# Tiles at byte 128 mod 512, and the latents' squares added some steps ahead of their sum

## The chip, the cores and the metric

The kernel runs on one core of a Trainium2 chip. The metric is the time of one execution on the device, in microseconds, as the median of three runs. One execution was also taken by the hardware profiler; all rows below come from it.

## What is computed

Two stacked models over 256 tokens of width 1024, all in float32. The reference, cut to its order:

```
h = x + gated_deltanet(rmsnorm(x))                 # 16 heads, chunks of 64
h = h + conv_gated_mlp(rmsnorm(h))                 # feed-forward 0, width 2816
k, v = shared_kv(h)
h = h + sliding_window_sink_attention(rmsnorm(h), k, v)
h = h + conv_gated_mlp(rmsnorm(h))                 # feed-forward 1
x = rmsnorm(h)
# second model
p = rms_norm(x) @ w_in           # linear attention q, k, v, gate; latents c_q (384), c_kv (256)
y_a = gla_branch(...) @ w_o_gla
y_b = mla_branch(rms_norm(c_q), rms_norm(c_kv), ...) @ w_o_mla
x = x + rms_norm((g_a * y_a + g_b * y_b) @ w_out)
x = x + rms_norm((silu(h @ w_fg) * (h @ w_fu)) @ w_fd)
```

Each latent is normalized by the root of the mean of its squares.

## The kernel before

**Matmuls.** Every float32 operand of a large product is held as two float32r parts, high and low, and a product is three matmuls into the same PSUM bank (`mm3`, lines 250 to 252): high x high, high x low, low x high. The first operand given is loaded into the array, the second one is moved through it. `gemm` loads weights (128 x 128) and moves activations of 256 columns (`xh`, `xl`; `fh`, `fl`; `ah`, `al`; `oh`, `ol`). `gemm_nat` and the last block's `down` load activations and move weights of 512 columns. Each such matmul loads its own operand, while the matmul before it is running.

**Weights.** All weights lie in one array `wall` of 362 tiles of 128 x 1024 float32, in the order of use. `_raw` (line 169) fetches a tile over SyncE's queue, `_prep` (line 176) splits it: ScalarE copies to `wh` (line 187), VectorE subtracts for `wl` (line 188). `w` (line 231) prepares two tiles ahead of the one in use (`LA = 2`), and each of `wr`, `wh`, `wl` has four buffers of 4,096 B per partition.

**Steps.** Work beside the matmuls (norms, attention, scans) is written as generators. `w` counts column tiles of weights; after each four of them `tick` lets every generator run to its next `yield`. So a `yield` is a distance of 12 matmuls of 256 columns in TensorE's order. The program is traced in that order, a scheduler orders the instructions of each engine by it, and each engine runs its own queue in order.

**Memory.** On-chip memory is handed out by pools, one behind the other in the order in which they are opened (`run`, line 557 on): `cp` (constants: `cols` of 592 float32, `ident` and `ones` of 128), `wp` (weights' buffers), `hp` (`h`), `sp` (small tiles, squares, row vectors), `xp` (`xh`, `xl`), then a stage's own pool: `gp` (delta rule), `xp2` and `fp0` (feed-forward 0), `sw` (attention), `lp`, `fp1` (feed-forward 1), `mp` (the second model's mixer), `f2` (its feed-forward). Within a pool tiles follow each other by tags; a tile takes its size per partition, rounded up to 32 B, times its buffers. `sp`, for example, holds `sqa` (2,048 B), `sq` (2 x 2,048), `dg` (1,024), `rsy` (4 x 256), `rst` (2 x 256), `rowb` (2 x 1,024), and some twenty pieces of 32 B, 11,296 B in all.

**Feed-forward 0 and 1** run the same function `ffn` (line 1033). After the fourth group of up-projections it alternates 48 matmuls of the up-projection (into `pb`) with 24 that accumulate the down-projection into `acc` (`acc_k`, moving operands `ah`, `al`). The pool holds three `fpad` (128 x 516 float32), then in feed-forward 0 `tbl` (64 B) and `oneh` (1,536 B), in feed-forward 1 three tiles of 1,024 B for the position tables, then `fy`, `ah`, `al`.

**The mixer's opening** (`mixer`, line 1291). `lat` (line 1338) writes the latents' squares by ScalarE (line 1342), two latents of 128 for `c_kv` (`sql[0]`, `sql[1]`), three for `c_q`. The generator `lat_stage` (line 1431) adds them up on VectorE (lines 1436, 1444, 1445), `colsum` (line 362) sums them over the partitions by TensorE with a column of ones (line 367), `rstd` makes the reciprocal root by a chain of small VectorE operations, `rows` turns it into a row by TensorE (line 453). The generator `la_stage` (line 1393) runs beside it: `rope` (line 1378), two pairs of gate matmuls (line 1404) with a `yield` after each, then logarithm, exponential and scan by ScalarE and VectorE, up to `e4`. The keys' generator multiplies by `e4` (line 1467) and transposes on TensorE (line 1473).

Of the kernel before, what the change touches and what calls it, by code (L numbers as in the profile page):

```python
# [2 lines left out]

# [1 line left out]

# [4 lines left out]
F32 = mybir.dt.float32  # L10
F32R = mybir.dt.float32r
BF16 = mybir.dt.bfloat16
I32 = mybir.dt.int32
AF = mybir.ActivationFunctionType
ALU = mybir.AluOpType
# [4 lines left out]
P = 128  # L20
# [24 lines left out]
NCOL = sum(v[1] for v in COLS.values())  # L45
# [62 lines left out]

CW = _cw_terms()

WARM = (5, 1, 3)
# [29 lines left out]
class Builder:  # L143
    LA = 2

    def __init__(self, tc, a, spec, dbg=None, upto=99):
        self.tc, self.nc, self.a, self.spec, self.dbg, self.upto = tc, tc.nc, a, spec, dbg, upto
        self.n = 0
        self.halves = {}
        self.raws = {}  # L150
        self.sides = []
        self.ticks = 0
        self.ready = True
        self.evq = []
        self.cs = None
        self.pins = {}
        self.extra = ()
# [399 lines left out]
    def run(self):  # L557
        nc, tc = self.nc, self.tc
        with ExitStack() as es:
            self.cp = es.enter_context(tc.tile_pool(name="cp", bufs=1))  # L560
            self.wp = es.enter_context(tc.tile_pool(name="wp", bufs=2))
            self.hp = es.enter_context(tc.tile_pool(name="hp", bufs=1))
            self.sp = es.enter_context(tc.tile_pool(name="sp", bufs=2))
            self.xp = es.enter_context(tc.tile_pool(name="xp", bufs=1))
            self.dp = es.enter_context(tc.tile_pool(name="dp", bufs=1, space=DRAM))
            self.ps = es.enter_context(tc.tile_pool(name="ps", bufs=8, space=PSUM))
            self.h = self.hp.tile([P, KD, T], F32, name="h")
            self.cols = self.cp.tile([P, NCOL], F32, name="cols")
            self.ident = self.cp.tile([P, P], F32, name="ident")
            for b in range(4):  # L570
                nc.sync.dma_start(self.h[:, 2 * b : 2 * b + 2], self.a["xT"][:, 2 * b : 2 * b + 2])
            nc.sync.dma_start(self.ident, self.cst("ident"))
            self._raw(0)
            nc.sync.dma_start(self.cols, self.a["cols"])
            self.ones = self.cp.tile([P, P], F32, name="ones")
            nc.gpsimd.memset(self.ones, 1.0)
            self.gdn()
            if self.upto < 2:
                return
            with tc.tile_pool(name="xp2", bufs=1) as self.xp2:  # L580
                self.ffn(0)
                if self.upto < 3:
                    return
                self.swa()
            if self.upto < 4:
                return
            with tc.tile_pool(name="lp", bufs=1) as self.lp:
                self.block2_consts()
                self.ffn(1)
                if self.upto < 5:  # L590
                    return
                self.block2()
# [6 lines left out]
    def gdn(self):  # L599
        nc, tc, sp = self.nc, self.tc, self.sp  # L600
        x = self.newx()
        self.sqs = []
        with tc.tile_pool(name="gp", bufs=1) as gp:

            wb = self.bank("warm")
            warm = lambda n, r: [nc.tensor.matmul(wb[:, 0 : r.shape[1]], self.ones, r, start=True, stop=True) for _ in range(n)]
            warm(WARM[0], self.ones)
            for b in range(4):
                self.add_sq(self.sqs, "sqa", b, lambda o: nc.scalar.activation(o, self.h[:, 2 * b : 2 * b + 2], AF.Square))
            cs = self.colsum(self.sqs)  # L610
            if PRE0:
                self._prep(0)
            rc = self.rstd(cs, D)
            warm(WARM[1], self.sqs[0])
            rb = self.rows(rc, psum=True)
            warm(WARM[2], self.h[:, 0])
            for i in range(8):
                t = gp.tile([P, T], F32, tag="t2", bufs=8, name="xn")
                op = nc.vector.scalar_tensor_tensor(t, self.h[:, i], self.col("a_norm", i), rb, ALU.mult, ALU.mult)
                nc.scalar.activation(x[0][:, i], t, AF.Copy)  # L620
                nc.vector.tensor_tensor(x[1][:, i], t, x[0][:, i].bitcast(F32), ALU.subtract)  # L621
                if i in PINS:
                    self.pins[PINS[i]] = op
                    self._prep(PINS[i])
            self.gdn_body(gp, x)
# [407 lines left out]
    def ffn(self, layer):  # L1033
        nc, tc, sp = self.nc, self.tc, self.sp
        x = self.x
        self.stats_rows(D)
        with tc.tile_pool(name=f"fp{layer}", bufs=1) as fp:
            padded = [fp.tile([P, 2, 2 + T], F32, tag=f"fpad{i}", name=f"fpad{i}") for i in range(3)]
            for t in padded:
                nc.gpsimd.memset(t[:, :, 0:2], 0.0)  # L1040
# [63 lines left out]
    def swa(self):  # L1104
        nc, tc, sp = self.nc, self.tc, self.sp
        xk, xq = self.x
        self.stats(D)
        with tc.tile_pool(name="sw", bufs=1) as ap:
            self.swa_body(ap, xk, xq)

    def swa_body(self, ap, xk, xq):
# [137 lines left out]

    def block2(self):  # L1250
        nc, tc, sp = self.nc, self.tc, self.sp
        with tc.tile_pool(name="mp", bufs=1) as mp:
            xm = self.mixer(mp)
        self.ffn2(xm)

# [34 lines left out]
    def mixer(self, mp):  # L1290
        nc, sp = self.nc, self.sp
# [41 lines left out]
        sql = [None] * 5  # L1333
# [97 lines left out]
        def lat_stage():  # L1431
            while sql[1] is None:
                yield
            for _ in range(3):
                yield
            nc.vector.tensor_tensor(sql[0], sql[0], sql[1], ALU.add)
            c = self.colsum(sql[0:1])
            nc.vector.tensor_tensor(rkv, self.rstd(c, 256, rc), rc, ALU.mult)
            yield
            rk_["b"] = self.rows(rkv)  # L1440
            st["rkv"] = 1
            while sql[4] is None:
                yield
            nc.vector.tensor_tensor(sql[2], sql[2], sql[3], ALU.add)
            nc.vector.tensor_tensor(sql[2], sql[2], sql[4], ALU.add)
            for _ in range(3):
                yield
            c = self.colsum(sql[2:3])
            nc.vector.scalar_tensor_tensor(rqs, self.rstd(c, 384, rc), 192 ** -0.5, rc, ALU.mult, ALU.mult)
            st["rqs"] = 1  # L1450

        self.side(la_stage())
        self.side(lat_stage())
        list(self.gemm("w_c", x, KD, [4, 0, 1, 2], evac_c))

# [284 lines left out]
    def ffn2(self, xm):  # L1740
        nc, tc, sp = self.nc, self.tc, self.sp
        stt = nc.vector.scalar_tensor_tensor
        with tc.tile_pool(name="f2", bufs=1) as fp:
            wrow = fp.tile([P, 2, D], F32, tag="wrow", name="wrow")
            nc.gpsimd.dma_start(wrow, self.a["wrow"].to_broadcast([P, 2, D]))
            mw = fp.tile([P, 2, D], F32, tag="mw", name="mw")
# [269 lines left out]
```

## Time and profile before

| | |
|---|---|
| median of 3 runs | 1205.18 us (1204.91 to 1206.57) |
| the profiled execution | 1206.04 us, span 1204.2 us |
| TensorE busy | 1166.8 us (97%), 9,308 matmuls |
| VectorE busy | 896.5 us (74%) |
| ScalarE busy | 689.4 us (57%) |
| weights moved | 362 x 512 KB, mean 171 GB/s over the span |

A matmul's record lasts longer than its distance to the next one, since matmuls are pipelined: a row of 0.28 us may be followed 0.12 us later by the next. So the cost of a matmul in a stream is read from starts, and busy time in a window is the time in which at least one is under way. The granted clock is given as a share of 2.4 GHz; 0.5 is 1.2 GHz.

### The profile page before, as it was taken

The numbers are of one execution on the slowest core, as the hardware profiler recorded it, in microseconds if no ns is written. First come the engines' busy times: TensorE is split into PE (matmuls) and PEld (weight loads), VectorE is DVE, ScalarE is ACT, GpSimd is POOL, SyncE is SP. The second block draws the span as 40 slices with busy tenths as digits, with TensorE's granted clock in tenths as the row PEclk, the third lists the DMA queues.
The fourth block names the chain that finished last, engine by engine and source line by source line (L and its number), as shares of the span: only waits on it lengthen the run. The fifth ranks groups of instructions, "written<-read, shape, count | busy, mean of one in ns | idle before, by whom it ended". The sixth has DMA issues, their size and how long they took to land.

```text
span 1204.2 us, 23264 instructions
## 1 busy us (share of the span) xinstructions
PE 1166.8 (97%) x9308; PEld 1102.7 (92%) x9308; DVE 896.5 (74%) x1645; ACT 689.4 (57%) x1172; POOL 24.7 (2%) x46
## 2 busy tenths in 40 slices
PE   6999999999999999989999999799999999999997
PEld 6989888999999999889999998689789998999996
DVE  5968977669877879879987879546666667665565
ACT  4786556546655556656655557546465555444443
POOL 2000000000000001000000000000000000000000
PEclk9999999999999999999999999799999999999999
DMA  6546375455665657435656555244245664566562
GB/s 211 191 134 202 120 224 179 140 164 164 218 191 190 187 189 244 132 101 172 196 190 192 183 186 177 70 156 142 88 150 184 192 216 153 174 191 188 185 192 86
DMA packets 68204, 206.00 MB, mean 171 GB/s; under 512 B 18085, under 2 KB 18229, under 8 KB 67840
## 3 DMA queue, kind: packets, MB, share of 16 engines
q1 hardware_dynamic: 65488, 194.77, 51.3%
q0 software_dynamic: 2608, 9.75, 2.3%
q8 instruction: 73, 1.20, 0.4%
q14 instruction: 35, 0.29, 0.1%
HBM read 199.75 MB, written 4.74 MB: 170 GB/s over the span
## 4 chain that ended last, share of the span: by engine, by line
PE 81%; DVE 11%; ACT 3%; issue 2%; DMA 1%; SPq 0%; DVEq 0%; ACTq 0%; POOLq 0%
PE pb L250 18%; PE pb L251 18%; PE pb L252 18%; PE acc L250 6%; PE acc L252 6%; PE acc L251 6%; DVE wl L188 3%; DVE cy L705 1%; DMA NT<-s 1%; DVE TI L817 1%; DVE fst L815 1%; ACT wh L187 0%; DMA ident<-cst 0%; ACT S L1178 0%; DVE fy L1053 0%
## 5 line engine op out<-in xcount | busy, mean ns | idle before, releaser
L188 DVE TENSOR_TENSOR wl<-wr,wh 128x1024 fp32r<-128x1024 f32 x362 | 441.9, 1223 | 193.7 <-ACT wh L187 192.8
L187 ACT ACTIVATE wh<-wr 128x1024 fp32r<-128x1024 f32 x362 | 381.7, 1057 | 319.6 <-issue 88.2
L250 PE MATMUL pb<-xh,wh 128*128 128x256 f32 x1224 | 346.4, 283 | 0.6 <-ACT xh L620 0.6
L251 PE MATMUL pb<-xl,wh 128*128 128x256 f32 x1224 | 343.1, 280 | 0.3 <-DVE xl L621 0.2
L252 PE MATMUL pb<-xh,wl 128*128 128x256 f32 x1224 | 342.8, 281 | 0.2 <-DVE wl L188 0.2
L250 PEld LDWEIGHTS pb<-xh,wh 128*128 128x128 f32 x1224 | 231.2, 189 | 3.1 <-issue 1.6
L251 PEld LDWEIGHTS pb<-xl,wh 128*128 128x128 f32 x1224 | 231.3, 189 | 0.9 <-DVE xl L621 0.4
L252 PEld LDWEIGHTS pb<-xh,wl 128*128 128x128 f32 x1224 | 231.0, 189 | 0.4 <-DVE wl L188 0.4
L250 PE MATMUL pb<-fh,wh 128*128 128x256 f32 x416 | 116.9, 282 | 0.0
L251 PE MATMUL pb<-fl,wh 128*128 128x256 f32 x416 | 116.1, 279 | 0.5 <-DVE fl L471 0.4
L252 PE MATMUL pb<-fh,wl 128*128 128x256 f32 x416 | 115.8, 279 | 0.0
L252 PE MATMUL acc<-ah,wl 128*128 128x256 f32 x352 | 98.1, 279 | 0.4 <-DVE wl L188 0.4
L251 PE MATMUL acc<-al,wh 128*128 128x256 f32 x352 | 98.2, 279 | 0.0
L250 PE MATMUL acc<-ah,wh 128*128 128x256 f32 x352 | 98.1, 279 | 0.0
L251 PEld LDWEIGHTS pb<-fl,wh 128*128 128x128 f32 x416 | 78.3, 188 | 1.5 <-DVE fl L471 0.8
L250 PEld LDWEIGHTS pb<-fh,wh 128*128 128x128 f32 x416 | 78.1, 188 | 1.3 <-issue 0.4
L252 PEld LDWEIGHTS pb<-fh,wl 128*128 128x128 f32 x416 | 78.2, 188 | 0.0
L1053 DVE SCALAR_TENSOR_TENSOR fy<-fpad,cols,fy 128x256 f32<-128x256 f32 x176 | 73.4, 478 | 0.0
L250 PE MATMUL pb<-wh,xh 128*128 128x512 f32 (+1 forms) x176 | 70.9, 405 | 0.0
L251 PE MATMUL pb<-wl,xh 128*128 128x512 f32 (+1 forms) x176 | 68.9, 391 | 1.5 <-DVE wl L188 1.5
L252 PE MATMUL pb<-wh,xl 128*128 128x512 f32 (+1 forms) x176 | 68.5, 389 | 0.0
L252 PEld LDWEIGHTS acc<-ah,wl 128*128 128x128 f32 x352 | 66.2, 188 | 0.6 <-DVE wl L188 0.6
(455 smaller groups left out, 2082.0 us busy)
## 6 DMA issues: line engine op xcount, KB each, us to landing
wr<-wall SPq DMA_DIRECT2D x362, 512.0 KB, 3.8
wzd<-zt POOLq DMA_DIRECT2D x8, 256.0 KB, 2.8
wzog<-wzd POOLq DMA_DIRECT2D x4, 512.0 KB, 4.3
bias<-bd POOLq DMA_DIRECT2D x4, 512.0 KB, 6.8
h<-xT SPq DMA_DIRECT2D x4, 256.0 KB, 4.1
h<-xT POOLq DMA_DIRECT2D x1, 1024.0 KB, 7.8
wrow<-wrow POOLq DMA_DIRECT2D x1, 1024.0 KB, 9.4
out_dram<-mw SPq DMA_DIRECT2D x4, 256.0 KB, 2.0
```

Of the source, the lines that this page charges most:

```text
L187: nc.scalar.activation(hi, r, AF.Copy)
L188: i = nc.vector.tensor_tensor(lo, r, hi.bitcast(F32), ALU.subtract)
L250: mm(out, ah, bh, start=start, stop=False, skip_group_check=skip)
L251: mm(out, ah, bl, start=False, stop=False, skip_group_check=skip)
L252: mm(out, al, bh, start=False, stop=stop, skip_group_check=skip)
L705: nc.vector.scalar_tensor_tensor(y[:, i, n:], u[:, : T - n], w(j), y[:, i, n:], ALU.mult, ALU.add)
L815: nc.vector.tensor_tensor(tmp, NT[:, j, j + 1 :].unsqueeze(2).to_broadcast([P, m, j + 1]), TI[:, j, 0 : j + 1].unsqueeze(1).to_broadcast([ ...
L817: nc.vector.tensor_tensor(TI[:, j + 1 :, 0 : j + 1], TI[:, j + 1 :, 0 : j + 1], tmp, ALU.add)
L1053: nc.vector.scalar_tensor_tensor(y[:, i], u[:, i, j : j + T], w(j), y[:, i], ALU.mult, ALU.add)
```

## The change

A class `Split` takes the place of most pools: a tile of 1,024 B or more goes to one pool, rounded up to a multiple of 512 B, a smaller one to a second pool behind it, which is filled up to a multiple of 512 B at the end. The tile that is used keeps its shape. `cols` gets 48 more columns, of which nothing is used. In `lat_stage` the first addition moves ahead of the yields, and both sums stand four yields later in place of three.

```diff
+LINE = 512
+class Split:
+    def __init__(self, big, small, nbufs):
+        self.big, self.small, self.nbufs, self.tags = big, small, nbufs, {}
+
+    def tile(self, shape, dtype, **kw):
+        item = 2 if dtype == BF16 else 4
+        n = math.prod(shape[1:])
+        if n * item < 1024:
+            self.tags[kw.get("tag", kw.get("name"))] = -(-n * item // 32) * 32 * kw.get("bufs", self.nbufs)
+            return self.small.tile(shape, dtype, **kw)
+        unit = LINE // item
+        m = -(-n // unit) * unit
+        if m == n:
+            return self.big.tile(shape, dtype, **kw)
+        t = self.big.tile([shape[0], m], dtype, **kw)[:, :n]
...
+    def fill(self, rest):
+        n = (rest - sum(self.tags.values())) % LINE
+        if n:
+            self.small.tile([P, n // 4], F32, tag="fill", bufs=1, name="fill")
+
+@contextmanager
+def split_pool(tc, name, bufs, rest=0):
+    with tc.tile_pool(name=name, bufs=bufs) as big, tc.tile_pool(name=name + "s", bufs=bufs) as small:
+        p = Split(big, small, bufs)
+        yield p
+        p.fill(rest)
...
-            self.sp = es.enter_context(tc.tile_pool(name="sp", bufs=2))
-            self.xp = es.enter_context(tc.tile_pool(name="xp", bufs=1))
+            self.sp = es.enter_context(split_pool(tc, name="sp", bufs=2, rest=0))
+            self.xp = es.enter_context(split_pool(tc, name="xp", bufs=1))
...
-            self.cols = self.cp.tile([P, NCOL], F32, name="cols")
+            self.cols = self.cp.tile([P, NCOL + 48], F32, name="cols")[:, :NCOL]
...
         def lat_stage():
             while sql[1] is None:
                 yield
-            for _ in range(3):
-                yield
             nc.vector.tensor_tensor(sql[0], sql[0], sql[1], ALU.add)
+            for _ in range(4):
+                yield
             c = self.colsum(sql[0:1])
...
             nc.vector.tensor_tensor(sql[2], sql[2], sql[3], ALU.add)
             nc.vector.tensor_tensor(sql[2], sql[2], sql[4], ALU.add)
-            for _ in range(3):
+            for _ in range(4):
                 yield
             c = self.colsum(sql[2:3])
```

The pools `xp2`, `lp`, `gp`, `fp0`, `fp1`, `sw`, `mp` and `f2` become split pools in the same way.

## Rows read from the trace of the kernel before

**Rows 1.** windows: start:end us, length, busy us (count) per engine, granted clock, DMA share, GB/s

```profile
272.00:462.00 190.00, 190.00 (x1635) 189.16 (x1634) 161.99 (x259) 117.17 (x182) 4.49 (x7) 1.00 0.60 191
746.00:750.20 4.20, 1.43 (x10) 1.26 (x8) 3.42 (x11) 2.62 (x6) 0.00 (x0) 0.87 0.55 164
750.20:769.50 19.30, 19.30 (x115) 16.96 (x114) 10.31 (x41) 11.55 (x16) 0.00 (x0) 0.76 0.20 60
769.50:778.50 9.00, 0.27 (x4) 0.06 (x2) 7.82 (x12) 3.62 (x4) 0.00 (x0) 0.70 0.48 158
```

**Rows 2.** waits of TensorE: engine, line, releaser, us in total, times, longest

```profile
PE kdt L1473 <- DVE kd L1467: 8.7, 1, 8.7
PE csum L367 <- DVE sql L1436: 2.8, 1, 2.8
```

**Rows 3.** windows of the matmuls into `acc` alone, feed-forward 0 and 1

```profile
272.00:462.00 190.00, 63.08 (x528) 1.00 0.60 191
541.00:729.00 188.00, 65.77 (x528) 1.00 0.59 186
```

**Rows 4.** timeline of TensorE, feed-forward 0 and 1: start us, us, instruction

```profile
300.79 0.28 PE L250 MATMUL acc<-ah,wh 128*128 128x256 f32 x1
302.83 0.28 PE L250 MATMUL acc<-ah,wh 128*128 128x256 f32 x1
...
569.85 0.28 PE L250 MATMUL acc<-ah,wh 128*128 128x256 f32 x1
571.62 0.28 PE L250 MATMUL acc<-ah,wh 128*128 128x256 f32 x1
```

**Rows 5.** timeline of TensorE, the output product of the linear attention

```profile
970.14 0.28 PE L250 MATMUL pb<-goh,wh 128*128 128x256 f32 x1
975.74 0.28 PE L250 MATMUL pb<-goh,wh 128*128 128x256 f32 x1
```

**Rows 6.** groups by line and shape, TensorE: instruction, count, busy us, mean ns, idle before

```profile
L250 PE MATMUL pb<-xh,wh 128*128 128x256 f32 x1224 | 346.4, 283 | 0.6 <-ACT xh L620 0.6
L250 PE MATMUL pb<-fh,wh 128*128 128x256 f32 x416 | 116.9, 282 | 0.0
L250 PE MATMUL pb<-wh,xh 128*128 128x512 f32 x160 | 66.2, 416 | 0.0
L250 PE MATMUL acc<-oh,wh 128*128 128x256 f32 x192 | 55.1, 291 | 2.0 <-ACT oh L467 2.0
```

**Rows 7.** timeline of TensorE, 512-column matmuls of the last block

```profile
993.55 0.40 PE L250 MATMUL pb<-wh,xh 128*128 128x512 f32 x1
995.65 0.40 PE L250 MATMUL pb<-wh,xh 128*128 128x512 f32 x1
...
1095.22 0.39 PE L250 MATMUL acc<-wh,ah 128*128 128x512 f32 x1
1096.36 0.39 PE L252 MATMUL acc<-wh,al 128*128 128x512 f32 x1
```

**Rows 8.** groups by line, VectorE, 272 to 462 us, then 541 to 729 us

```profile
L1053 DVE SCALAR_TENSOR_TENSOR fy<-fpad,cols,fy 128x256 f32<-128x256 f32 x88 | 36.7, 477 | 0.0
...
L1053 DVE SCALAR_TENSOR_TENSOR fy<-fpad,cols,fy 128x256 f32<-128x256 f32 x88 | 36.7, 479 | 0.0
```

**Rows 9.** timeline of ScalarE at the latents' squares

```profile
747.43 0.64 ACT L1342 ACTIVATE sql<-pb 128x256 f32<-128x256 f32 x2
```

**Rows 10.** chain that ended last, 745 to 780 us: start us, us, step

```profile
747.56 1.23 DVE wl L188
748.78 0.35 DVE sql L1436
749.27 0.98 PE csum L367 x4
759.64 1.07 PE gate L1404 x4
778.49 1.11 PE kdt L1473 x4
```

More of the change, by code (lines that the diff above doesn't have):

```diff
@@ L1 @@
 import math
-from contextlib import ExitStack
+from contextlib import ExitStack, contextmanager
 import numpy as np
@@ L109 @@
 CW = _cw_terms()
+LINE = 512
[13 more added lines that the diff above has]
+        t = self.big.tile([shape[0], m], dtype, **kw)[:, :n]
+        if len(shape) == 2:
+            return t
+        ax = "abc"[: len(shape) - 1]
+        return t.rearrange("p (" + " ".join(ax) + ") -> p " + " ".join(ax), **dict(zip(ax, shape[1:])))
+    def fill(self, rest):
[8 more added lines that the diff above has]
+        p.fill(rest)
 WARM = (5, 1, 3)
@@ L579, in run @@
                 return
-            with tc.tile_pool(name="xp2", bufs=1) as self.xp2:
+            with split_pool(tc, name="xp2", bufs=1) as self.xp2:
                 self.ffn(0)
@@ L586, in run @@
                 return
-            with tc.tile_pool(name="lp", bufs=1) as self.lp:
+            with split_pool(tc, name="lp", bufs=1) as self.lp:
                 self.block2_consts()
@@ L602, in gdn @@
         self.sqs = []
-        with tc.tile_pool(name="gp", bufs=1) as gp:
+        with split_pool(tc, name="gp", bufs=1) as gp:
             wb = self.bank("warm")
@@ L1036, in ffn @@
         self.stats_rows(D)
-        with tc.tile_pool(name=f"fp{layer}", bufs=1) as fp:
+        with split_pool(tc, name=f"fp{layer}", bufs=1) as fp:
             padded = [fp.tile([P, 2, 2 + T], F32, tag=f"fpad{i}", name=f"fpad{i}") for i in range(3)]
@@ L1107, in swa @@
         self.stats(D)
-        with tc.tile_pool(name="sw", bufs=1) as ap:
+        with split_pool(tc, name="sw", bufs=1) as ap:
             self.swa_body(ap, xk, xq)
@@ L1251, in block2 @@
         nc, tc, sp = self.nc, self.tc, self.sp
-        with tc.tile_pool(name="mp", bufs=1) as mp:
+        with split_pool(tc, name="mp", bufs=1) as mp:
             xm = self.mixer(mp)
@@ L1433, in lat_stage @@
                 yield
-            for _ in range(3):
+            nc.vector.tensor_tensor(sql[0], sql[0], sql[1], ALU.add)
+            for _ in range(4):
                 yield
-            nc.vector.tensor_tensor(sql[0], sql[0], sql[1], ALU.add)
             c = self.colsum(sql[0:1])
@@ L1742, in ffn2 @@
         stt = nc.vector.scalar_tensor_tensor
-        with tc.tile_pool(name="f2", bufs=1) as fp:
+        with split_pool(tc, name="f2", bufs=1) as fp:
             wrow = fp.tile([P, 2, D], F32, tag="wrow", name="wrow")
```

## Prediction

> **What bounds the kernel now.** I read the stages first, then the TensorE spacing, then the two places where TensorE stops. In the stage table [rows 1] the first feed-forward block is typical of most of the kernel: in 190 us TensorE is busy for all 190, VectorE for 162, ScalarE for 117. So the time of such a stage is the number of its matmuls times the distance from one matmul's start to the next (its pitch), and whatever does not change that pitch or that number is hidden. The list of waits [rows 2] has only two over 2.5 us after the start of the kernel, both in the third block's opening: 2.8 us at the column sum of the latents' squares (line 367, waiting for the VectorE addition of line 1436) and 8.7 us at line 1473. The layout part of the change can only act through the pitch, the latents part only through the first of these waits.
>
> **Where the tiles lie now.** This is arithmetic on the code. With 48 more columns `cols` takes 2,560 B = 5 x 512 and the constants' pool 3,584 B = 7 x 512, and the change says that the weights then lie at 128 mod 512; so `cols` begins at 128, and today the weights begin 2,368 + 512 + 512 = 3,392 B later, at 448 mod 512. `h` too. The pool `sp` then adds 11,296 B (22 x 512 + 32), which puts `xh`, `xl` and all later 8 KB tiles at 480. In feed-forward 0 the three `fpad` (2,080 B each as allocated), `tbl` (64 B) and `oneh` bring `ah`, `al` to 128; in feed-forward 1, where `tbl` and `oneh` are missing, they lie at 64. In the last block `ah`, `al` lie at 192. After the change all of them, and the weights, lie at 128.
>
> **The layout, priced by the trace itself.** The two feed-forward blocks run the same 528 accumulating matmuls, same shapes, same weights' buffers at 448, and differ in where the moving operand lies: 128 in the first, 64 in the second. In the first they occupy 63.08 us, in the second 65.77 us [rows 3]: 2.7 us, or 5.1 ns a matmul. Starts show the same: 300.79 to 302.83 is 18 matmuls, 113.3 ns each; 569.85 to 571.62 is 15, 118 ns each [rows 4]. Operands at 480 stand between: 970.14 to 975.74 is 48 matmuls at 116.7 ns [rows 5]. I read this as: a 256-column matmul whose moving operand lies at 128 costs 113.3 to 113.9 ns, I take 113.6, and the change puts every one of them there. That the new tiles meet weights at 128 and not 448 no row shows; the nearest are 512-column matmuls, below.
>
> The sum. Moving operand at 480 and loaded weights at 448: 1,224 + 416 groups of three lines (250 to 252), and 192 more with `oh`, which lie at 256 and 352 and which I take at the same price [rows 6]: (1,224 + 416 + 192) x 3 = 5,496 matmuls x (116.7 - 113.6) = 17.0 us. The 528 of feed-forward 1: 2.7 us. In the 512-column matmuls the weights are the moving operand. Where `xh` at 480 is loaded, 993.55 to 995.65 holds 9 at 233 ns; where `ah` at 192 is loaded, 1095.22 to 1096.36 holds 5 at 228 ns [rows 7]. There are 160 x 3 = 480 of the former [rows 6]; 5.5 ns each is 2.6 us. Smaller groups of these kinds are left out. Together 22.3 us.
>
> VectorE gains nothing: the 88 multiply-adds of line 1053 take 477 ns with tiles at 128 and 479 ns with tiles at 64 [rows 8], and VectorE and ScalarE are below TensorE anyway. Transfers keep their sizes and order, but each 512 KB weight tile must come some 2.5% sooner; TensorE's stages are not held by them now (191 GB/s at 60% of the DMA engines' time [rows 1]), so I price that at nothing, and at some 3 us if the cover goes. Padding adds no instruction. Not all of the 22.3 us comes home: the stages with chains through VectorE (the delta-rule block, the attention) have steps set by latency, and where VectorE already fills 162 of 190 us it will fill 162 of some 185. I keep nine tenths: **20 us**. The bounds are zero (addresses count for nothing where weights and moving tiles lie alike) and 27 us (the small groups too, and all of it realized).
>
> The Trainium skill says otherwise. Its page "SBUF — State Buffer", section "Who interferes with whom", gives TensorE two independent read ports and lets only the port pair shared by VectorE and GpSimd cause contention. The Trainium skill's page "TensorE: Matmul & The Clock Gate", section "Back-to-back issue gap", gives N/2.4 + 2.5 ns for a warm matmul, 109.2 ns at 256 columns, without a term for addresses. By these the layout would be worth 0 us; this trace does not agree, with 2.7 us between two like sets of 528 matmuls [rows 3].
>
> **The latents' squares.** Now the addition of line 1436 stands in front of its column sum in the same step; it starts at 748.78, right after a 1.23 us weight subtraction, and the sum at 749.27, after TensorE has stood for 2.8 us [rows 2, 10]. TensorE then ran at half its clock: 0.87 granted in 746 to 750.2 and 0.76 in 750.2 to 769.5 [rows 1], which is 0.26 x 4.2 + 0.48 x 19.3 = 10.4 us at 1.2 GHz. In the change the addition is traced three steps sooner and the sum one step later (four yields for three; a step is 4 column tiles, 12 matmuls, 1.4 us). The squares are written by ScalarE from 747.43, two in 0.64 us [rows 9], so the addition can be done by about 748.2, and TensorE arrives at about 747.9 in place of 746.5 (749.27 less 2.8): some 0.5 us of wait is left with the sum's start, 2.3 are saved. Because the addition comes sooner, VectorE's queue may hold behind it the weight subtraction that now starts at 747.56 [rows 10], by some 0.6 us; TensorE uses that tile two tiles later, so nobody waits. If the short stop does not bring the clock down, the half-clock stretch goes too: at most half of 10.4 us, 5.2, of which I take 3, since the column sum's own VectorE steps (some 4 us of small operations behind it) then stand closer to TensorE's use of them. What counts in the end is how much sooner the second pair of gate matmuls runs (759.64 to 760.71), because from its end a chain of ScalarE and VectorE steps leads to line 1473 at 778.49 [rows 10], 17.8 us that nothing in the change shortens. The wait there stays near 9 us, and the clock falls after it as today. The second addition group only gains a step on a sum that nothing waited for. Taken: 2.3 + 3 = **5 us**; bounds 0 (the stop moves to the next row sum) and 2.8 + 5.2 = 8 us.
>
> **Sum.** The profiled execution took 1206.04 us with a span of 1204.2 us. Less 20 + 5 it gives 1181.0 us; the median of the runs shown, 1205.18, is 0.9 us below the profiled one, so I predict **1180 us**.
>
> **Rivals.**
> - *The layout does nothing* (chance 0.12). The pitch belongs to something else that differs between the blocks; every tile pair lying alike leaves 116.7 ns. For it: no row shows 256-column matmuls with both tiles lying alike. Against it: two like sets with two pitches [rows 3, 4], where I find nothing but the places that differs. Time: the latents' part alone, 1200 us, or 1205 if that fails too. By the two sections of the Trainium skill named above, it would go this way.
> - *Lying alike is the bad case* (0.11), the one that ends slower. Not the place of the moving tile counts but its distance to the weights that are loaded at the same time: 192 B in feed-forward 0 (good), 128 B in feed-forward 1 (bad), 32 B for `xh` (between). The change makes it 0 everywhere, which no row shows for 256 columns. If 0 is as bad as 128 (113.6 + 5.1 = 118.7 ns): 5,496 x (118.7 - 116.7) + 528 x (118.7 - 113.6) = 13.7 us more, less 2.6 at 512 columns and less 5 for the latents: 1211 us. It decides from a pitch of about 118 ns on. Against it: at 512 columns distances of 256 B are good, and only tiles at 480 bad.
> - *The stop at the latents moves* (0.17, the layout working). TensorE then waits at the row sum for the column sum's VectorE steps, or the clock falls all the same: 1185 us. It lies within the forecast's range.
> - *The producers become the bound* (0.08): with TensorE quicker, VectorE or the weights' transfers hold half of the gain in the feed-forward stages: 1190 us.
>
> The forecast itself has 0.52. **Range**: the low end is all 27 us and 8 us, 1170, less some 4 us for loads that gain from lying at 128 too: 1166. The high end takes in the first rival with the latents' part: 1202. What lies outside is mostly the slower rival. A measurement of this kernel can tell about 0.2%, 2.4 us, from no change. Faster by more: forecast, moved stop and producers (0.77) and half of the first rival (0.06): 0.83; within it 0.06; slower 0.11.
>
> **What the profile after would show.** Right: starts of `xh`, `fh`, `oh` and layer 1 `acc` matmuls 113 to 114 ns apart, equal occupation for the 528 matmuls of both feed-forward blocks, 228 ns at 512 columns with `xh`, VectorE's durations unchanged, no wait over 1 us at line 367 for the latents, and full clock from there to line 1473. Wrong: 116.7 ns unchanged (first rival), 118 and more (second), a new wait at the row sum, or waits of TensorE on `wl` in the feed-forward blocks.

## The result and the profile after

The kernel after takes 1215.99 us (median; 1212.45 to 1217.03), the kernel before, run beside it, 1205.88 us (1204.91 to 1208.21). The ratio is 1.0076 with a 95% interval of 1.0050 to 1.0101: the change makes the kernel 0.8% slower, 10 us, where 25 us less were forecast. The profiled execution took 1215.82 us; its span is 1213.7 us against 1204.2.

Lines of the kernel after stand 40 further down: 250 to 252 are now 290 to 292, 188 is 228, 367 is 407, 1473 is 1513.

The plainest view is a count of matmuls in a stretch in which TensorE never stops. Two stretches of 60 us lie inside the two feed-forward blocks, in all versions shown here: 310 to 370 us and 610 to 670 us. Columns are start:end, length, then busy us and count of TensorE, of its weight loads, of VectorE, ScalarE and GpSimd, granted clock, share of the DMA engines, GB/s. The kernel before:

```profile
310.00:370.00 60.00, 60.00 (x520) 60.00 (x520) 48.51 (x74) 34.56 (x51) 0.00 (x0) 1.00 0.63 202
610.00:670.00 60.00, 60.00 (x514) 60.00 (x513) 47.36 (x72) 34.11 (x50) 0.00 (x0) 1.00 0.61 188
```

The kernel after, the same view:

```profile
310.00:370.00 60.00, 60.00 (x503) 60.00 (x502) 47.01 (x71) 33.46 (x49) 0.00 (x0) 1.00 0.64 194
610.00:670.00 60.00, 60.00 (x502) 60.00 (x501) 46.52 (x71) 33.46 (x49) 0.00 (x0) 1.00 0.57 182
```

A count takes in some two or three matmuls that began ahead of the stretch, so the pitch (the distance from one start to the next) is 60 us over the count less 2.5: 115.9 and 117.3 ns before, 119.9 and 120.1 after, at full clock and with TensorE busy for all 60 us in both. VectorE and ScalarE were busy for less of the same time, and the transfers moved less (194 and 182 GB/s in place of 202 and 188): they are not what slows it. The starts say the same (timeline of TensorE, kernel after; start us, us, instruction): 39 matmuls in 4.68 us are 120.0 ns each, and in contrast to [rows 4, 5] the kernel after has this one value in all its stages: the mean of every group of 256-column matmuls at full clock (of 20 or more) lies between 119.5 and 120.0 ns.

```profile
599.82 0.28 PE L290 MATMUL pb<-xh,wh 128*128 128x256 f32 x1
...
604.50 0.28 PE L290 MATMUL pb<-xh,wh 128*128 128x256 f32 x1
```

The groups that answer to [rows 6] and [rows 8] (line, engine, instruction, count, busy us, mean ns of one, idle before). The `xh` group went from 346.4 to 349.6 us, `fh` from 116.9 to 118.4, while 512 columns went down from 66.2 to 65.5; VectorE's multiply-add is unchanged at 478 ns:

```profile
L290 PE MATMUL pb<-xh,wh 128*128 128x256 f32 x1224 | 349.6, 286 | 0.2 <-ACT xh L660 0.2
L290 PE MATMUL pb<-fh,wh 128*128 128x256 f32 x416 | 118.4, 285 | 0.0
L1093 DVE SCALAR_TENSOR_TENSOR fy<-fpad,cols,fy 128x256 f32<-128x256 f32 x176 | 73.4, 478 | 0.0
L290 PE MATMUL pb<-wh,xh 128*128 128x512 f32 x160 | 65.5, 412 | 0.0
L290 PE MATMUL acc<-oh,wh 128*128 128x256 f32 x192 | 56.4, 299 | 2.0 <-ACT oh L507 2.0
```

At 512 columns with `xh` loaded, which [rows 7] had at 233 ns, the timeline now has 9 matmuls in 2.04 us, 227 ns each:

```profile
999.98 0.39 PE L290 MATMUL pb<-wh,xh 128*128 128x512 f32 x1
...
1002.02 0.39 PE L290 MATMUL pb<-wh,xh 128*128 128x512 f32 x1
```

The waits of TensorE answer to [rows 2]. The wait of line 407 for the latents' sum (`sql`) is gone from the list; the one for `sqa` is another, at the kernel's start, and the one at line 1513 stays:

```profile
PE kdt L1513 <- DVE rky L395: 8.3, 1, 8.3
PE csum L407 <- DVE sqa L593: 6.3, 1, 6.3
PE acc L290 <- ACT oh L507: 2.0, 1, 2.0
```

And the stretches around the latents, which answer to [rows 1]: full clock up to the stop at line 1513 (775 to 784 us), where 0.87 and 0.76 were granted before.

```profile
745.00:775.00 30.00, 30.00 (x237) 28.48 (x236) 24.94 (x76) 24.93 (x41) 0.00 (x0) 1.00 0.52 164
775.00:784.00 9.00, 0.73 (x5) 0.65 (x4) 9.00 (x21) 3.62 (x4) 0.00 (x0) 0.79 0.31 109
```

So the latents' part and the 512 columns went the way that the prediction said, and the loss is in one number: a 256-column matmul takes 120.0 ns in place of 113.9 to 118.5. That is the reading of the second rival ("lying alike is the bad case"), at a higher price than it had.

### The profile page after: what moved, and what is told of

Its sections match the earlier page's. It is cut to its first block, busy times and chain, and to the rows that moved or that the text cites. A ratio compares the mean times of both kernels' runs of the same rounds, so it can differ in the third digit from the quotient of the medians.

```text
span 1213.7 us, 23265 instructions
## 1 busy us (share of the span) xinstructions
PE 1182.5 (97%) x9308; PEld 1122.9 (93%) x9308; DVE 899.3 (74%) x1645; ACT 688.5 (57%) x1172; POOL 20.4 (2%) x46
## 4 chain that ended last, share of the span: by engine, by line
PE 91%; DVE 6%; ACT 1%; DMA 1%; issue 1%; SPq 0%; DVEq 0%; ACTq 0%
PE pb L290 21%; PE pb L291 20%; PE pb L292 20%; PE acc L290 7%; PE acc L292 7%; PE acc L291 7%; DVE wl L228 1%; DMA wr<-wall 1%; PE pt L1251 1%; PE ssb L764 1%; DMA ident<-cst 0%; PE s L1195 0%; DVE cy L745 0%; ACT wh L227 0%; PE kv L1662 0%
## 5 line engine op out<-in xcount | busy, mean ns | idle before, releaser
L290 PE MATMUL pb<-xh,wh 128*128 128x256 f32 x1224 | 349.6, 286 | 0.2 <-ACT xh L660 0.2
L292 PE MATMUL pb<-xh,wl 128*128 128x256 f32 x1224 | 346.3, 283 | 0.7 <-DVE wl L228 0.7
L290 PEld LDWEIGHTS pb<-xh,wh 128*128 128x128 f32 x1224 | 234.7, 192 | 2.7 <-issue 1.3
L291 PEld LDWEIGHTS pb<-xl,wh 128*128 128x128 f32 x1224 | 234.7, 192 | 0.7 <-DVE xl L661 0.4
L292 PEld LDWEIGHTS pb<-xh,wl 128*128 128x128 f32 x1224 | 234.5, 192 | 0.9 <-DVE wl L228 0.9
L290 PE MATMUL pb<-fh,wh 128*128 128x256 f32 x416 | 118.4, 285 | 0.0
L292 PE MATMUL pb<-fh,wl 128*128 128x256 f32 x416 | 117.5, 283 | 0.0
```

The source lines that it names most:

```text
L290: mm(out, ah, bh, start=start, stop=False, skip_group_check=skip)
L291: mm(out, ah, bl, start=False, stop=False, skip_group_check=skip)
L292: mm(out, al, bh, start=False, stop=stop, skip_group_check=skip)
```

## The experiments

### Which quantity sets the pitch: place or distance

The 120 ns fit two theories. **Distance** (theory A below): what counts is moving place minus loaded place, which the change made 0. **Place** (theory B): a tile's own place counts, and weights at 128 are bad. No row of either kernel separates them, so the first run is a benchmark of matmuls alone: one loaded and one moving operand, no other engine at work. In the cut below, `p` is the place of the loaded operand, and the moving one lies 32 x `d` bytes further on.

```diff
+PLACES = (128, 448, 0, 64, 256, 320)
...
+            for p in PLACES:
+                for d in range(16):
+                    last = stream("d" + LET[d] + "q", p, 32 * d)
```

> This kernel leaves out the whole model: it only runs streams of 24 matmuls (8 groups of three, 256 moving columns, float32r, one PSUM tile a stream). Six places of the loaded operand (byte 128, 448, 0, 64, 256, 320 mod 512), each with the moving operand 0, 32, 64 ... 480 bytes further on (tiles daq to dpq), then 16 streams of 512 columns with the loaded operand at 128 (waq to wpq). Theory A, distance: the pitch of a matmul is set by moving minus loaded place mod 512 alone, so that all six rounds over the places give one table: 0 bytes 120.0 ns, 32 bytes 116.8, 128 bytes 118.5, 192 bytes 113.9, 320 bytes 117.9, 416 bytes 117.7 (the pairs that the two kernels' traces show), whatever the loaded place is. Theory B, place: an operand's own place sets it. With the loaded operand at 128 every distance then costs about 120 ns, with it at 448 the moving places have the prices of the kernel before (64: 118.5, 128: 113.9, 256: 117.9, 352: 117.7, 480: 116.8). Theory C, neither: all streams have one pitch, and the 120.0 ns of the kernel after come from something else that the change moved.

Starts of streams of 24 matmuls, from the timeline of this run; each stream begins where the one ahead of it ends. The loaded operand is at 128, the distances are 0 (`daq`), 192 (`dgq`) and 256 (`diq`):

```profile
66.65 0.28 PE L58 MATMUL daq<-xh,wh 128*128 128x256 f32 x1
...
69.53 0.28 PE L58 MATMUL dbq<-xh,wh 128*128 128x256 f32 x1
...
83.73 0.28 PE L58 MATMUL dgq<-xh,wh 128*128 128x256 f32 x1
...
86.45 0.28 PE L58 MATMUL dhq<-xh,wh 128*128 128x256 f32 x1
...
89.29 0.28 PE L58 MATMUL diq<-xh,wh 128*128 128x256 f32 x1
...
92.16 0.28 PE L58 MATMUL djq<-xh,wh 128*128 128x256 f32 x1
```

The same with the loaded operand at 448:

```profile
111.92 0.28 PE L58 MATMUL daq<-xh,wh 128*128 128x256 f32 x1
...
114.79 0.28 PE L58 MATMUL dbq<-xh,wh 128*128 128x256 f32 x1
...
128.99 0.28 PE L58 MATMUL dgq<-xh,wh 128*128 128x256 f32 x1
...
131.72 0.28 PE L58 MATMUL dhq<-xh,wh 128*128 128x256 f32 x1
...
134.55 0.28 PE L58 MATMUL diq<-xh,wh 128*128 128x256 f32 x1
...
137.42 0.28 PE L58 MATMUL djq<-xh,wh 128*128 128x256 f32 x1
```

A stream of distance 0 takes 2.88 and 2.87 us (120 ns a matmul), one of 192 takes 2.72 and 2.73 us (113.5), one of 256 takes 2.87 us in both (119.6). The place of the loaded operand changes nothing. The mean distances between starts inside a stream, which agree within 0.6 ns over all six places:

| moving minus loaded, bytes mod 256 | 0 | 32 | 64 | 96 | 128 | 160 | 192 | 224 |
|---|---|---|---|---|---|---|---|---|
| 256 columns, ns | 119.6 | 118.0 | 118.0 | 119.6 | 118.7 | 117.4 | 113.7 | 118.0 |
| 512 columns, ns (loaded at 128) | 227 to 230 | 233.5 | 229.6 | 234 | 234 | 234 | 233 | 233 |

Distances 256 bytes apart have the same value at 256 columns. So it is the distance, mod 256, and place and theory C fall. At 512 columns the order is another: there, distance 0 is the best. In all six rounds a distance follows the same other distance; what another stream ahead does is asked further down.

### The change without the weights' part

The kernel after, with the weights put back to where they were before and only the moving tiles at 128: a distance of 192.

```diff
+            self.hp.tile([P, 48], F32, tag="hpad", name="hpad")
             self.h = self.hp.tile([P, KD, T], F32, name="h")
...
             self.ones = self.cp.tile([P, P], F32, name="ones")
+            self.cp.tile([P, 80], F32, tag="cpad", name="cpad")
```

> The kernel after with one thing changed: the weights' buffers lie at byte 448 mod 512 and not at 128 (80 float32 of padding ahead of them in one pool, 48 in the other); all moving tiles stay at 128, so that moving minus loaded is 192 bytes. Theory A (distance) and theory B (place) both expect the pitch of the first feed-forward of the kernel before, 113.9 ns, in nearly all 7050 matmuls of 256 columns, against 120.0: 7050 x 6.1 = 43 us less than the kernel after, about 1173 us, 0.973 of the kernel before; the matmuls of 512 columns stay at 227 to 228 ns. Theory C (the price has nothing to do with where weights and moving tiles lie against each other): 120.0 ns and 1216 us.

Measured: 1186.9 us (1182.7 to 1192.2), 0.9834 of the kernel before (0.9808 to 0.9860). It beats both kernels, by 20 and by 29 us. The stretches of the first section, and two more:

```profile
310.00:370.00 60.00, 60.00 (x532) 60.00 (x531) 49.13 (x76) 35.97 (x53) 0.00 (x0) 1.00 0.64 205
...
610.00:670.00 60.00, 60.00 (x532) 60.00 (x531) 48.25 (x74) 34.85 (x51) 0.00 (x0) 1.00 0.60 196
870.50:885.50 15.00, 15.00 (x129) 15.00 (x128) 10.14 (x14) 10.43 (x12) 0.00 (x0) 1.00 0.62 200
```

In the two stretches of the feed-forward blocks the pitch is 60 / 529.5 = 113.3 ns, close to the 113.9 expected. But from 870.5 to 885.5 us it is 15 / 126.5 = 118.6 by the count, 117.8 by the starts, at the same distance, and the second feed-forward itself begins with 117.8 (544 to 572 us by the starts). Over all 6,930 such matmuls the mean is 114.9 and not 113.9, 7 us, about half of the 14 us by which the run missed its 1173; another 1 us are the 512 columns (230.0 ns on the mean, 228.7 in the kernel after), and part of the rest lies in the first 240 us: there, 2,000 TensorE instructions, 964 matmuls of 256 columns among them, end 1.9 us sooner than in the kernel after, where 6.1 ns for each of these would be 5.9. At one distance there are two pitches.

### Each half of the change alone

The kernel before with the latents' change alone:

```diff
-            for _ in range(3):
-                yield
             nc.vector.tensor_tensor(sql[0], sql[0], sql[1], ALU.add)
+            for _ in range(4):
+                yield
             c = self.colsum(sql[0:1])
...
             nc.vector.tensor_tensor(sql[2], sql[2], sql[4], ALU.add)
-            for _ in range(3):
+            for _ in range(4):
                 yield
```

> The kernel before with the latents' change alone (squares added up some steps ahead of their sums, no tile moved). My reasons: the wait of 2.8 us at the column sums goes, and with it the stretch of 10.2 us at half clock behind it, in all 5 to 7.5 us: about 1199 us, ratio 0.994 to 0.996; every matmul of 256 columns keeps its pitch of before (116.8 ns with the moving tile at 480 and the loaded one at 448). Rival: the stretch at half clock comes back elsewhere, or the next wait takes the place: 1203 to 1206 us.

Measured: 1197.9 us (1196.9 to 1201.0), ratio 0.9931 (0.9909 to 0.9953), 9 us less. The wait of 2.8 us is gone, and the stretch up to the stop runs at full clock:

```profile
739.00:762.00 23.00, 22.51 (x177) 20.88 (x176) 18.63 (x68) 19.23 (x32) 0.00 (x0) 1.00 0.47 154
```

By the interval the gain is 5.7 to 11 us; of the 5 to 7.5 expected it holds the upper part, and the medians' 9 lie above them. The two profiles give the place: the last matmul ahead of the former stop starts at 746.22 us before and at 745.60 here, line 1473 at 778.49 and at 769.9, so 8.0 us of the gain arise between the two.

The kernel after with the latents' lines of before, so the layout alone:

> The kernel after without the latents' change (layout alone). By the sum over matmuls, 5325 x 3.2 us/1000 at the pair 480/448 plus 528 x 6.1 at the pair 128/448, less 480 x 5 at 512 columns, the layout costs 17 + 3 - 2 = 18 us or a little more: 1224 us, ratio 1.015, with the wait of about 2.8 us at the column sums and the stretch at half clock behind it as in the kernel before. Rival: the layout's own cost is only the 10 us by which the kernel after is slower, and the latents' change gave nothing: 1216 us. Where the new stretch at half clock of 6.8 us (531 to 538 us in the kernel after) shows here as well, it is the layout's.

Measured: 1222.1 us (1220.1 to 1224.8), ratio 1.0128 (1.0101 to 1.0154), 15 us more. The sum said 18, which lies in the interval (12 to 19). The two waits of [rows 2] are both there, the one at the column sum too:

```profile
PE kdt L1513 <- DVE kd L1507: 8.5, 1, 8.5
PE csum L407 <- DVE sql L1476: 2.8, 1, 2.8
```

So the two parts work against each other: layout +15, latents -9, together +10 in the kernel after, which their intervals allow.

Where the layout costs nothing is the delta-rule block. In the first 240 us, with 964 of the 256-column matmuls, TensorE gets as far with the layout as without it, at full clock and with stops between its streams. The kernel before, then the layout alone:

```profile
0.00:240.00 240.00, 226.84 (x1999) 208.39 (x2000) 185.40 (x435) 151.27 (x305) 16.52 (x27) 1.00 0.56 175
0.00:240.00 240.00, 228.30 (x2002) 210.90 (x2002) 186.50 (x437) 151.01 (x305) 12.26 (x27) 1.00 0.54 175
```

The half-clock stretch at 531 to 538 us of the kernel after (0.51 granted) was put to neither part:

```profile
527.00:531.00 4.00, 2.07 (x16) 1.17 (x16) 2.91 (x6) 4.00 (x17) 0.00 (x0) 1.00 0.75 230
531.00:538.00 7.00, 6.05 (x28) 6.05 (x29) 4.01 (x13) 1.88 (x5) 0.00 (x0) 0.51 0.29 95
```

With the layout alone it does not show. With the latents alone there is a shorter one at the same work, though up to there that kernel's instructions and places are those of before:

```profile
519.00:524.00 5.00, 2.12 (x17) 1.35 (x15) 3.46 (x10) 4.33 (x19) 0.00 (x0) 1.00 0.76 224
524.00:528.00 4.00, 4.00 (x23) 3.98 (x22) 2.86 (x9) 0.98 (x2) 0.00 (x0) 0.57 0.29 113
```

It lies behind the stop at the end of the attention, which all versions have. So it can come with nothing of the change ahead of it. Of the eleven profiles of whole kernels here, nine show it, for 3.4 or 6.8 us, also that of the kernel before with its weights moved (below); the kernel before and the layout alone do not. How often it comes in one and the same kernel, one profile of each can't say. In a comparison of two single profiles I estimate it at half its length, 1.7 or 3.4 us.

### Two more tests of the distance in the whole kernel

The kernel after with the weights at 384 (paddings of 64 and 64 float32): a distance of 256 bytes, none of the weights at 128.

> The kernel after with the weights at byte 384 mod 512, all moving tiles at 128: a distance of 256 bytes. Theory A, distance mod 256 as in the micro-benchmark: this is the same as no distance, 120.0 ns in nearly all 7050 matmuls of 256 columns, 227 to 229 ns at 512, and 1216 us as the kernel after has (ratio 1.008), though no weight lies at 128. Theory B, that weights at 128 are the bad place in the whole kernel: less than 119 ns and under 1210 us.

Measured: 1215.2 us (1214.1 to 1217.7), ratio 1.0079 (1.0065 to 1.0092). Pitch and time are those of the kernel after (x502, 60 / 499.5 = 120.1 ns):

```profile
310.00:370.00 60.00, 60.00 (x502) 60.00 (x501) 47.69 (x71) 33.12 (x50) 0.00 (x0) 1.00 0.61 193
610.00:670.00 60.00, 60.00 (x502) 60.00 (x502) 46.54 (x71) 33.45 (x49) 0.00 (x0) 1.00 0.58 183
```

The kernel before with its weights alone moved to 128 (paddings of 48 and 80 float32):

> The kernel before with the weights alone moved, to byte 128; every moving tile stays where it was (xh, xl and the later tiles at 480, ah and al at 128, 64 and 192), and the latents' squares too. Theory A, distance mod 256, priced by the micro-benchmark: 5325 matmuls go from a distance of 32 to one of 96, 116.8 to 119.8 ns, +16 us; 528 of the first feed-forward from 192 to 0, 113.9 to 120, +3 us; 528 of the second from 128 to 192, 118.5 to 113.3 or 117.8, -0.4 to -2.7 us; 512 columns +1 us: about 1225 us, ratio 1.016. Rival, that the moving tiles' shift and not the weights' made the kernel after slow: 1206 us, 116.8 ns.

Measured: 1223.4 us (1222.9 to 1226.8), ratio 1.0150 (1.0136 to 1.0163). The prices of the bare benchmark gave 1225. The starts of the 528 matmuls of feed-forward 1, now at 192, lie 114.0 ns apart (118.5 before), those of feed-forward 0, now at 0, 119.7 (113.9 before): the two blocks have changed sides though `ah` and `al` have not moved.

### Why one distance has two pitches

Theory D: the pitch at 192 bytes is a state that a stream falls into when it begins and then keeps. Theory E: other traffic slows those stretches. A second benchmark, again with nothing else running, puts four matmuls of another width ahead of each stream:

```diff
+KICKS = (32, 64, 96, 128, 160, 224, 384, 512)
...
+            for d in range(16):
+                for j, c in enumerate(KICKS):
+                    kick(c, j)
+                    last = stream("d" + LET[d] + LET[j] + "q", 128, 16 * d)
```

> This kernel leaves out the whole model. Streams of 24 matmuls (256 columns) with the loaded operand at 128 and the moving one 0, 16, 32 ... 240 bytes further on, each run eight times, each time behind four matmuls of another width (32, 64, 96, 128, 160, 224, 384, 512 columns), which leave TensorE at another point of its cycle; then 512 columns in the same way behind two widths. It asks why the version with the weights at 448 ran 12 us over its 1173: there, at one and the same distance of 192 bytes, whole stretches ran at 113.3 ns (573 to 720 us) and others at 117.8 (991 to 1165 us). Theory D, a state with memory: at 192 bytes some widths leave a stream at 113.3 ns and others at 117.8, and it stays there to its end; at 0 bytes every stream has 120 or close to it. Theory E, traffic: the 117.8 ns come from the other engines or the DMA of those stages, so that here, where nothing else runs, every stream of 192 bytes has 113.3 to 113.7 ns whatever ran before it. At steps of 16 bytes the best distance lies at 192 or next to it; another one that has 113 to 115 ns behind all eight widths would be the better place for the weights.

Two streams of distance 192, behind 32 columns (`dmaq`) and behind 64 (`dmbq`). The rows are every third matmul:

```profile
392.00 0.28 PE L58 MATMUL dmaq<-xh,wh 128*128 128x256 f32 x1
...
393.36 0.28 PE L58 MATMUL dmaq<-xh,wh 128*128 128x256 f32 x1
...
395.21 0.28 PE L58 MATMUL dmbq<-xh,wh 128*128 128x256 f32 x1
...
396.62 0.28 PE L58 MATMUL dmbq<-xh,wh 128*128 128x256 f32 x1
```

12 matmuls take 1.36 us in one (113.3 ns) and 1.41 us in the other (117.5; 117.8 over the stream's last nine). The mean over the last nine starts of each stream, ns:

| width ahead | 32 | 64 | 96 | 128 | 160 | 224 | 384 | 512 |
|---|---|---|---|---|---|---|---|---|
| distance 0 | 120.0 | 120.0 | 120.0 | 120.0 | 120.0 | 120.0 | 120.0 | 120.0 |
| distance 32 | 116.8 | 117.8 | 116.6 | 116.8 | 117.8 | 117.5 | 116.8 | 116.7 |
| distance 64 | 117.9 | 117.9 | 117.8 | 117.8 | 117.9 | 117.8 | 117.9 | 117.8 |
| distance 112 | 113.2 | 113.2 | 113.2 | 113.4 | 113.4 | 113.4 | 113.2 | 113.4 |
| distance 192 | 113.4 | 117.8 | 117.9 | 113.4 | 117.8 | 113.4 | 113.2 | 113.4 |

That is theory D: at 192 five of eight widths leave 113.3 ns and three 117.8, with no other traffic at all, so theory E falls. Other distances have more than one pitch too (116.6 to 117.8 ns at 32, 113.4 to 119.3 at 144). At 112, which is not next to 192 as was expected, every stream ended at 113.3, so the next run tried it.

The weights at 272, the moving tiles at 128, so 112 mod 256:

```diff
-        hi = self.wtile(j, F32R, "wh")
-        lo = self.wtile(j, F32R, "wl")
+        if j in self.extra:
+            hi = self.wtile(j, F32R, "wh")
+            lo = self.wtile(j, F32R, "wl")
+        else:
+            o = 4 + 1024 * (self.nw % 4)
+            self.nw += 1
+            hi = self.wall[:, o : o + 1024]
+            lo = self.wall[:, 4096 + o : 4096 + o + 1024]
```

> The kernel after with the weights' high and low parts at byte 272 mod 512 (one tile of eight slices, begun 16 bytes into it, so that a place off the grid of 32 bytes can be had); all moving tiles stay at 128: moving minus loaded is 112 mod 256, the one distance at which all eight streams of the micro-benchmark settled at 113.2 to 113.4 ns, whatever ran before. Theory D (some distances have two pitches and a stream keeps the one that it fell into): the stretches at 117.8 ns of the version with the weights at 448 (527 to 573, 870 to 899, 991 to 1165 us) fall to about 113.5 to 114.5, 7000 x about 1.2 ns = 8 to 9 us less, and the 736 matmuls of 512 columns lose about 2.5 ns each (at the distance the other way round, 144), 2 us: about 1180 us, ratio 0.978. Theory E (those stretches are slow because of what else runs in them): they stay at 117.8 and the time is 1187 to 1189 us.

Measured: 1214.8 us (1210.1 to 1221.2), ratio 1.0079 (1.0050 to 1.0108): both expectations missed. The pitch is 119.9 ns in the first feed-forward and 116.6 in the second:

```profile
310.00:370.00 60.00, 60.00 (x503) 60.00 (x502) 46.79 (x71) 33.09 (x50) 0.00 (x0) 1.00 0.60 193
610.00:670.00 60.00, 60.00 (x517) 60.00 (x516) 47.95 (x71) 33.50 (x49) 0.00 (x0) 1.00 0.60 190
```

In the benchmark the loaded operand lay at 128 and the moving one at 240; here the loaded one lies at 272 and the moving one at 128. The first benchmark had shown that only the distance counts for places that are multiples of 32 bytes, and the step to 16 took that for granted, and with it that 112 and 112 + 256 are alike there. That did not hold in the whole kernel. Which of the two fails was not tried, nor whether moving tiles at 240 would have 113.3 ns there.

The last three runs test theory D in the whole kernel: the version with the weights at 448, with one narrow matmul put ahead of each of the 20 groups of the last block's loop, of the product `w_om` (moving tiles `yoh` and `yol`) and of a group in the second feed-forward.

```diff
+    def kick(self, b, w, x):
+        self.nc.tensor.matmul(b[:, 0:32], w, x[:, 0:32], start=True, stop=True, skip_group_check=True)
...
+                        if i == 0 and k == 0:
+                            self.kick(b, wh, xh[:, 0])
```

> The version with the weights at 448, with 22 matmuls of 32 columns added: one ahead of each of the 20 groups of 48 matmuls of 256 columns in the last block's loop, where each follows 12 matmuls of 512 columns and runs at 117.8 ns (1020 to 1165 us), one ahead of the first group of the product w_om (870 to 899 us, 117.8 ns) and one in the second feed-forward. They write columns that the group behind them starts anew. Theory D, a state with memory: the added matmul changes the point in the cycle at which the stretch begins; where that is the right one, the 48 matmuls fall to 113.3 ns, 48 x 4.5 = 0.21 us a group, 4.3 us in the 20 groups less 20 x 0.03 us for the added ones, and 1.1 us in w_om: 1182 us; where it is the wrong one they stay at 117.8 and the time is 1187 to 1188. At least one of the widths 32, 64 and 96 should turn them. Theory E, other engines' or DMA traffic in those stages: 117.8 ns with all three widths.

> As with 32 columns, but the 22 added matmuls have 64 columns, about 0.06 us each. Theory D: the groups of the last block's loop at 113.3 ns and 1183 us, or at 117.8 and 1188 us, whichever the point of the cycle gives, not a value between; theory E: 117.8 ns.

> As with 32 columns, but the 22 added matmuls have 96 columns, about 0.09 us each. Theory D: the groups of the last block's loop at 113.3 ns and 1184 us, or at 117.8 and 1189 us, whichever the point of the cycle gives, not a value between; theory E: 117.8 ns.

Measured: 1196.3 us (32 columns), 1188.3 (64) and 1191.3 (96); ratios 0.9916 (0.9888 to 0.9943), 0.9845 (0.9816 to 0.9874), 0.9874 (0.9835 to 0.9913). Stretches of 60 us in the second feed-forward and of 15 us in w_om. With 32 columns:

```profile
610.00:670.00 60.00, 60.00 (x512) 60.00 (x511) 47.65 (x71) 33.47 (x49) 0.00 (x0) 1.00 0.60 189
881.00:896.00 15.00, 15.00 (x129) 15.00 (x129) 10.02 (x14) 10.24 (x12) 0.00 (x0) 1.00 0.63 203
```

With 64:

```profile
610.00:670.00 60.00, 60.00 (x532) 60.00 (x531) 48.43 (x74) 35.11 (x53) 0.00 (x0) 1.00 0.61 194
872.00:887.00 15.00, 15.00 (x134) 15.00 (x134) 10.09 (x14) 10.34 (x12) 0.00 (x0) 1.00 0.59 202
```

With 96:

```profile
610.00:670.00 60.00, 60.00 (x511) 60.00 (x511) 47.51 (x71) 34.14 (x50) 0.00 (x0) 1.00 0.59 185
880.00:895.00 15.00, 15.00 (x134) 15.00 (x134) 10.10 (x14) 10.34 (x12) 0.00 (x0) 1.00 0.58 203
```

In w_om the stretch behind the added matmul runs at 113.3 ns in place of 117.8 with 64 or 96 columns (x129 to x134), not with 32; the transfers and the other engines are as before. The second group of the last block's loop says the same: by its starts it has 113.7 and 113.5 ns with 64 and 96 columns, 117.8 with 32. That the width decides was not repeated, as each version has one profile, but two places agree on it.

In the second feed-forward the same work runs at 113.3 (x532) or 117.8 (x512, x511). This the added matmul did not decide: right behind it, at 547 us, the version with 64 columns has 117.8 too, and takes up 113.3 for good only at 582 us, behind later breaks of its stream. With 32 columns the slower pitch holds without a break from 552 to 731 us. About 1,230 matmuls lie in the longest unbroken part with 96 columns, 585 to 730 us; at 4.5 ns that is 5.5 us, most of the 8 us between the spans of these profiled executions with 64 and with 96 columns (1186.9 and 1195.1 us; 1197.0 with 32).

That a pitch can differ between two executions with nothing changed, the first stages show. The version with the weights at 448 and the one with 64 columns have the same TensorE order and the same places up to 546 us, where the first added matmul stands. Yet 24 to 36 us after the start one runs at 113.4 ns and the other at 117.8 by the starts:

```profile
24.00:36.00 12.00, 12.00 (x108) 12.00 (x108) 9.57 (x16) 7.28 (x11) 2.40 (x1) 1.00 0.82 267
24.00:36.00 12.00, 12.00 (x104) 12.00 (x103) 9.55 (x16) 7.07 (x12) 2.82 (x1) 1.00 0.83 273
```

What missed: but for that second group the last block's loop stayed at 117.8 ns or above with all three widths, so the 4.3 us there did not come; the times with 32 and 96 columns lie above both values expected of them; and none of these versions is better than the one with the weights at 448 alone.

## Why the prediction was wrong, point by point

- **What bounds the kernel, and where the tiles lie**: right. The loss is pitch times number in stages where TensorE never stops, and the places worked out on the code give the pitches measured at 0, 96 and 256 bytes. They do not fix the pitch at 192 bytes, which has two, nor in the version with the weights at 272.
- **The price of the layout**: the step that failed is "a 256-column matmul whose moving operand lies at 128 costs 113.3 to 113.9 ns ... and the change puts every one of them there". [Rows 3 to 5] show three pairs (128 and 448, 64 and 448, 480 and 448), all with the weights at 448. Place and distance fit these alike; I took the place and carried it to weights at 128, a pair that the text itself said no row shows. What the runs showed in its place is that the distance counts: with the weights left at 448 the change would have made it 192, with 113.3 or 117.8 ns; moving them too made it 0, with 120.0, beside 96 the worst in the table.
- **The sum with the right prices**: 5,325 matmuls from 116.8 to 120.0 are +17.0 us, 528 of feed-forward 0 from 113.9 to 120.0 +3.2, 528 of feed-forward 1 from 118.5 to 120.0 +0.8, 550 with `oh` from about 117.8 +1.2, about 480 of 512 columns from 233.2 to 228.7 -2.1: +20 us where the prediction had -22. The layout alone measured +15. Some 3 of the other 5 are the 964 matmuls of the first 240 us (3.2 ns each), which cost no time there: the delta-rule block, as the prediction said, has steps that the pitch does not set. The rest was not isolated.
- **512 columns**: right, 227 ns in place of 233, about 2 us.
- **VectorE, ScalarE, transfers**: right that they neither gain nor lose; 478 ns against 477 and 479 [rows 8].
- **The latents**: right in mechanism (the wait at the column sum and the half-clock stretch behind it both went; the wait at line 1513 stayed) and low in size: 5 us taken, 9 measured alone (5.7 to 11 by the interval). The term that was mis-sized is the clock: 3 of 5.2 us were taken for the stretch behind the stop, and all of it came, with full clock from 739 to 762 us. Between the stop and line 1473 the profiles have 8.0 us of gain, which is the upper bound that the text gave, 2.8 + 5.2; the last us of the 9 is not explained.
- **The rivals**: "lying alike is the bad case" is what happened. Its price was 118.7 ns, as if 0 were no worse than 128 bytes; it is 120.0, with which the rival's own sum gives some 1220 us; that 1216 was measured is in part the latents' larger gain. What spoke against it in the text, that at 512 columns a distance of 256 is good, is true and does not carry over: the two widths rank the distances differently.
- **The weight of the rivals**: two readings fitted the same rows, and one had 0.52 and more, the other 0.11. Nothing in the trace justified that: each explained all three pairs with as many assumptions. The range ended at 1202 and so left out the one case that the rows had priced least.

## What to carry to other kernels

Where a trace shows a cost that moves with an address, list every pair of operands that it shows and ask whether a sum, a difference or one place alone explains it; if one operand never moved, the rows can't tell, and a change that moves it has no price yet. Tiles "all lying alike" is a choice of distance 0 for operands that are read together, and here a bad one: with the moving tiles alone at 128 the kernel is 29 us faster than with the weights there too. Change the distance between two operands by a padding and look at the pitch in one long stretch before the whole layout follows.

## What the runs showed of the hardware

- At 256 columns of float32r and full clock the pitch depends on moving minus loaded place, mod 256 bytes: 113.3 ns to some 120 ns among multiples of 32, the same for six places of the loaded operand behind the same stream. The Trainium skill's page "TensorE: Matmul & The Clock Gate", section "Back-to-back issue gap", gives N/2.4 + 2.5 ns as the gap of a warm matmul taken by itself, by which I estimate 109.2 ns for this width. No settled stream of the runs here lies below 113.2 ns.
- Some distances have more than one pitch. At 192 bytes a stream runs at 113.3 or 117.8 ns and was seen to keep its pitch until it is broken off, in one run for 179 us (552 to 731 us). Which of the two it takes went with the width run ahead of it in the benchmark, and differed between two executions with the same places and the same order in the whole kernel. The runs of the version with the weights at 448 spread from 1182.7 to 1192.2 us, those of the kernel after from 1212.5 to 1217.0. That the wider spread comes from this state is likely and was not shown, as only one execution of each is profiled.
- For operands off the 32-byte grid the distance mod 256 alone does not fix the pitch: 113.2 to 113.4 ns with the loaded one at 128 and the moving one at 240, 116.6 to 120 with 272 and 128, both 112 bytes apart mod 256.
- What inside TensorE or its memory ports makes the distance count is open: the runs show when it costs, not why, and the "cycle" of the expectations is a picture that no run shows.
